# Value and gate transpositions emitted in the middle of the next projection chain

## The chip, the cores and the metric

The kernel runs on one core of a Trainium2 chip. The metric is the device time of that core in microseconds. The engines are PE (matrix products, with PEld for its weight loads), DVE, ACT and POOL (elementwise work), and SP, which issues all of this kernel's DMAs, in order, from one queue.

## The reference

The reference is one transformer block in float32 on 1024 positions of width 1024: a gated feed-forward layer, a mixing layer, a second feed-forward layer and a norm. The mixing layer projects the normed input with one wide matrix and runs two kinds of attention:

```
proj = h @ w_in
(q_da, k_da, v_da, q_ns, kc_raw, vc_raw, ks_raw, vs_raw, kw_raw, vw_raw, g_ns, g_a, g_b) = split(proj)
y_da = diff_attention(q_da, k_da, v_da, ...)          # 8 heads, values 128 wide
y_ns = nsa(q_ns, kc_raw, ..., vw_raw, g_ns, ...)      # 16 heads, 3 branches, gates
merged = sigmoid(g_a) * (y_da @ w_proj_da) + sigmoid(g_b) * (y_ns @ w_proj_nsa)
return merged @ w_out
```

What matters here are the values `v_da` (differential attention), `vs_raw` and `vw_raw` (two branches of the second attention) and the gates `g_ns`. They are computed with the channel on the partitions and are needed with the position on the partitions, so they are transposed.

## The kernel before

Every float32 product is done in three products of rounded parts: high weight by high input, high by low, low by high (`mm3`, lines 49 to 51). A *chain* is the 24 such matmuls that give one tile of 128 channels by 512 positions: 8 blocks of the width, 3 each. The positions are handled in two halves, `tb` 0 and 1.

The *preliminary units* (from 667 us) each load one or two weight tiles, split them on ACT (high part, line 86) and DVE (low part, line 82), run a chain for each half, and finish it:

- `raw_unit` stores the inputs of a compression; `rope_pair` does queries and keys: products with cosines and sines on DVE, sums on POOL, a split into `rh` and `rl`, and stores.
- `v_da_unit` (values of one head of the differential attention) scales the chain's result into `vt` (line 570), transposes it on PE in four pieces into `tr` (line 573), splits it into `vh` and `vl`, and stores both (line 578).
- `v_ns_unit` does the same for the second attention (lines 588 and 591), `g_unit` for the gates (lines 623 and 626), with an exponential and a reciprocal behind it.

`prelim` runs these up to the queries of the second attention; between them stand the compression products (`hid`, lines 700 to 702). `da_phase` first runs six more units (two for heads 0 and 1, four for heads 2 and 3, the last two of them value units), then opens the buffers of the attention and goes through the heads. There each step computes scores `S` (line 791, two buffers), their maximum on DVE (line 798) and exponentials `Pt` on ACT (line 800), transposes the probabilities (line 846) and multiplies them with values (`o`, lines 868 to 870). Between the steps a *filler* (`K.fill`) emits pieces of the remaining projection units, with weights loaded at line 1057 and split at line 1067.

In `v_da_unit` the tile `vt` has the tag `m13`, `vh` the tag `rh` and `vl` the tag `rl` of a pool with one buffer a tag; `rope_pair` uses the same tags. So a `vh` can be written only when the store of the `vh` or `rh` before it has landed.

The program's order is not the order on the engines: the framework's scheduler sorts the instructions by their place in the program (as a priority) and by its own estimate of times, and then each engine works through its list in order. Buffers are assigned in the same step.

Of the kernel before, what the change touches and what calls it, by code (L numbers as in the profile page):

```python
# [7 lines left out]
F32 = mybir.dt.float32  # L8
F32R = mybir.dt.float32r
AF = mybir.ActivationFunctionType  # L10
ALU = mybir.AluOpType
# [4 lines left out]
P = 128  # L16
T = 1024
TB = 512
NTB = 2
HB = 256  # L20
D = 1024
KD = 8
# [25 lines left out]
def mm3(nc, out, w, wk, x, start, stop, skip=False):  # L48
    first = nc.tensor.matmul(out, lhsT=w[0][:, wk], rhs=x[0], start=start, stop=False, skip_group_check=skip)  # L49
    nc.tensor.matmul(out, lhsT=w[0][:, wk], rhs=x[1], start=False, stop=False, skip_group_check=skip)  # L50
    nc.tensor.matmul(out, lhsT=w[1][:, wk], rhs=x[0], start=False, stop=stop, skip_group_check=skip)  # L51
    return first
# [6 lines left out]
def fill_gemm(K, out, w, xs):  # L59
    for k in range(KD):  # L60
        if K.low:
            with K.tc.high_priority(offset=-K.low):
                first = mm3(K.nc, out, w, k, xs[k], k == 0, k == KD - 1)
        else:
            first = mm3(K.nc, out, w, k, xs[k], k == 0, k == KD - 1)
        if K.gate is not None:
            K.tc.add_manual_dep(first.ins, K.gate.ins.name,
                                mybir.DependencyInfo(mybir.DependencyClass.NoSync, mybir.DependencyReason.DATA),
                                reason="pace the filler")
        if K.fill is not None:  # L70
            K.fill.tick(first)
        yield


def drain(units):
    for u in units:
        for _ in u:
            pass


def lo_of(nc, lo, src, hi):
    return nc.vector.tensor_tensor(out=lo, in0=src, in1=hi.bitcast(F32), op=ALU.subtract)  # L82


def split(nc, hi, lo, src):
    nc.scalar.activation(out=hi, in_=src, func=AF.Copy)  # L86
    return lo_of(nc, lo, src, hi)


def load_w(K, src):  # L90
    if K.fill is not None:
        return K.fill.take()
    return load_w_parts(K, src, 1)()
# [469 lines left out]
def v_da_unit(K, h):  # L563
    nc = K.nc
    w = load_w(K, K.A["win"][C_VDA + h])
    for tb in range(NTB):
        ps = K.gm.tile([P, TB], F32, tag="gm", name="gm")
        yield from fill_gemm(K, ps, w, K.h[tb])
        vt = K.mp.tile([P, TB], F32, tag="m13", name="vt")
        nc.vector.tensor_tensor(out=vt, in0=ps, in1=K.R[tb], op=ALU.mult)  # L570
        tr = K.gm.tile([P, 4, P], F32, tag="gm", name="tr")
        for j in range(4):
            nc.tensor.transpose(tr[:, j], vt[:, j * P:(j + 1) * P], K.ident)
        vh = K.mp.tile([P, 4, P], F32R, tag="rh", name="vh")
        vl = K.mp.tile([P, 4, P], F32R, tag="rl", name="vl")
        split(nc, vh, vl, tr)
        for hl, t in ((0, vh), (1, vl)):
            nc.sync.dma_start(out=K.s_v[h][hl][:, tb * 4:tb * 4 + 4], in_=t.bitcast(F32))


def v_ns_unit(K, br):
    nc = K.nc
    w = load_w(K, K.A["win"][C_V2 + br])
    for tb in range(NTB):
        ps = K.gm.tile([P, TB], F32, tag="gm", name="gm")
        yield from fill_gemm(K, ps, w, K.h[tb])
        vt = K.mq.tile([P, TB], F32, tag="vt", name="vt")
        nc.vector.tensor_tensor(out=vt, in0=ps, in1=K.R[tb], op=ALU.mult)
        tr = K.tr.tile([P, 4, P], F32, tag="tr", name="tr")
        for j in range(4):  # L590
            nc.tensor.transpose(tr[:, j], vt[:, j * P:(j + 1) * P], K.ident)
        vv = K.mq.tile([P, 2, 4, 2, 64], F32R, tag="vv", name="vv")
        for g in range(2):
            split(nc, vv[:, g, :, 0], vv[:, g, :, 1], tr[:, :, g * 64:(g + 1) * 64])
            nc.sync.dma_start(out=K.s_v2[br][g][:, tb * 4:tb * 4 + 4],
                              in_=vv[:, g].rearrange("p j a d -> p j (a d)").bitcast(F32))


def raw_unit(K, kv, w=None):
# [16 lines left out]
def g_unit(K):  # L616
    nc = K.nc
    w = load_w(K, K.A["win"][C_G])
    for tb in range(NTB):
        ps = K.gm.tile([P, TB], F32, tag="gm", name="gm")  # L620
        yield from fill_gemm(K, ps, w, K.h[tb])
        vt = K.mq.tile([P, TB], F32, tag="vt", name="vt")
        nc.vector.tensor_tensor(out=vt, in0=ps, in1=K.R[tb], op=ALU.mult)
        tr = K.tr.tile([P, 4, P], F32, tag="tr", name="tr")
        for j in range(4):
            nc.tensor.transpose(tr[:, j], vt[:, j * P:(j + 1) * P], K.ident)
        gs = K.G[:, tb * 4:tb * 4 + 4]
        nc.scalar.activation(out=gs, in_=tr[:, :, 0:48], func=AF.Exp, scale=-1.0)
        nc.vector.tensor_scalar(out=gs, in0=gs, scalar1=1.0, scalar2=None, op0=ALU.add)
        nc.vector.reciprocal(out=gs, in_=gs)  # L630
    for i in range(8):
        nc.vector.tensor_scalar(out=K.Gc[:, i], in0=K.G[:, i].rearrange("p (h b) -> p h b", b=3)[:, :, 0],
                                scalar1=K.rowv[:, i:i + 1], scalar2=None, op0=ALU.mult)


def gate_unit(K, c):
# [558 lines left out]
def da_units(K, p):  # L1195
    return [lambda: rope_pair(K, C_QDA + 2 * p, K.s_q[p]), lambda: rope_pair(K, C_KDA + 2 * p, K.s_k[p]),
            lambda: v_da_unit(K, 2 * p), lambda: v_da_unit(K, 2 * p + 1)]
# [27 lines left out]
def da_phase(K, cg):  # L1225
    nc = K.nc
    with ExitStack() as ctx:
        K.kp, K.vp, K.qp = open_pool(K, ctx, "dk", B_DK), open_pool(K, ctx, "dv", B_DV), open_pool(K, ctx, "dq", B_DQ)
        K.nk, K.vv = {}, {}
        for n, f in enumerate(da_units(K, 0)[:2] + da_units(K, 1)):  # L1230
            if n == 2:
                early = da_load_parts(K, 0)
            if n >= 2:
                next(early)
            if n == 5:
                q0 = da_queries(K, 0, 0)
            drain([f()])
        cg.close()
        K.low = LOW_DA
        log_exp(K)  # L1240
        K.pp, K.sm, K.tp, K.op = (open_pool(K, ctx, "dp", B_DP), open_pool(K, ctx, "dsm", 6), open_pool(K, ctx, "dt", B_DT),
                                  open_pool(K, ctx, "do", 1))
        K.sp = open_pool(K, ctx, "sp1", 2, True)
        K.tr = open_pool(K, ctx, "tr1", TR_DA, True)
        K.ops = open_pool(K, ctx, "o1", 1, True)
        K.gm = open_pool(K, ctx, "gm1", 3 - TR_DA, True)
        pend = K.fin = None

        def finish(h, m, res):
            if m % 2 == 0:  # L1250
                K.o = K.ops.tile([P, TB], F32, tag="o", name="o")
            if K.fin:
                da_finish2(K, *K.fin)
                K.fin = None
            da_pv(K, h, m, res, K.o)
            if m % 2 == 1:
                K.fin = da_finish(K, h, m // 2, K.o)

        ng = NG_DA // 2
        W = K.A["win"]  # L1260
        units = []
        for p in (2, 3):
            cs = [[C_QDA + 2 * p, C_QDA + 2 * p + 1], [C_KDA + 2 * p, C_KDA + 2 * p + 1], [C_VDA + 2 * p], [C_VDA + 2 * p + 1]]
            units += [(f, [W[c] for c in ws]) for f, ws in zip(da_units(K, p), cs)]
        units += [(f, [W[C_GATE + c]]) for c, f in enumerate(gate_units(K, range(16)))]
        units += [(lambda d=d: pda_unit(K, d), [K.A["wda"][d]]) for d in range(KD)]
        fill = K.filler = Filler(K, units)
        for p in range(4):
            fill.pace(4 * (p + 1) if p < 2 else 8 + ng * (p - 1), PACE_DA)
            for h in (2 * p, 2 * p + 1):  # L1270
                if h:
                    da_load(K, h)
                for m in range(4):
                    qt = q0 if h + m == 0 else da_queries(K, h, m)
                    if h == 4:
                        ns_load_key(K, m)
                    res = da_scores(K, h, m, qt, fill.step)
                    if pend:
                        finish(*pend)
                    pend = (h, m, res)  # L1280
            fill.end()
        finish(*pend)
        da_finish2(K, *K.fin)
# [108 lines left out]
def body(tc, A, out):  # L1392
    nc = tc.nc
    K = Ctx()
    K.tc, K.nc, K.A = tc, nc, A
    K.low, K.vv, K.gate, K.fill, K.seen = 0, {}, None, None, {}
    K.h, K.acc, K.R = [None] * 2, [None] * 2, [None] * 2
    with ExitStack() as ctx:
# [172 lines left out]
```

## Time and profile before

| | us |
|---|---|
| median of 3 runs | 2966.28 |
| lowest, highest | 2965.57, 2974.5 |
| profiled execution | 2967.67 |
| its span in the trace | 2965.9 |
| busy: PE / DVE / ACT / POOL | 2862.2 / 1974.1 / 1268.8 / 975.4 |
| mean granted clock of PE | 0.991 |

PE is busy for 97% of the span, at close to full clock. The busy times are sums over stages that differ, so what an idle time is worth has to be read in its own stage. In the trace a row of a timeline names the line, the engine, the tiles written and read, and in brackets how long the engine had stood idle before and what released it.

### The profile page before, as it was taken

Reading aid. Unit: us, or ns where it says so; the run is one execution under the profiler, and the core shown is the slowest. Engines: PE = TensorE matmul, PEld = TensorE weight load, DVE = VectorE, ACT = ScalarE, POOL = GpSimd, SP = SyncE. Lnnn points to the kernel's source line nnn. Section 1 sums busy time; section 2 is a strip of 40 time slices with the busy share of each in tenths; the row PEclk is TensorE's granted clock in tenths of the full one; section 3 lists DMA queues with packets and bytes.
Section 4 is the critical chain, followed back from the end, with each engine's and each line's share of the span. In section 5 each row is a group of like instructions: output and inputs, shape, how many; then the busy total and the mean of one; then the engine's idle time right before and its main releaser. Section 6 shows DMA issues by size and latency. Waiting matters only on the chain.

```text
span 2965.9 us, 39981 instructions
## 1 busy us (share of the span) xinstructions
PE 2862.2 (97%) x14238; PEld 2392.2 (81%) x14238; DVE 1974.1 (67%) x3140; ACT 1268.8 (43%) x2195; POOL 975.4 (33%) x765
## 2 busy tenths in 40 slices
PE   9999999999999899989899999999999999999998
PEld 7877878888888678778788888888778888778886
DVE  8775666666587467667777777776433866676556
ACT  6322224442233245445566666666433432223343
POOL 4366651000144123222233332223242436655001
PEclk9999999999999999999999999999999999999999
DMA  4355557655456544444332234222742145455854
GB/s 139 114 190 180 181 196 273 216 179 171 151 199 222 184 162 164 175 165 163 127 122 70 85 127 154 79 82 72 299 148 96 64 149 206 163 178 197 280 181 147
DMA packets 212711, 478.19 MB, mean 161 GB/s; under 512 B 20897, under 2 KB 39585, under 8 KB 212513
## 3 DMA queue, kind: packets, MB, share of 16 engines
q1 hardware_dynamic: 212512, 475.65, 47.0%
q8 instruction: 112, 1.84, 0.3%
q14 instruction: 87, 0.70, 0.1%
HBM read 313.56 MB, written 162.00 MB: 160 GB/s over the span
## 4 chain that ended last, share of the span: by engine, by line
PE 68%; DMA 11%; DVE 9%; POOL 4%; issue 4%; ACT 3%; SPq 1%; DVEq 0%; ACTq 0%; POOLq 0%
PE gm L49 6%; PE S L791 6%; PE gm L50 6%; PE gm L51 6%; PE Y L324 5%; PE acc L51 5%; PE acc L49 5%; PE acc L50 5%; PE tr L846 4%; PE X L324 3%; PE Z L324 3%; PE o L1004 2%; DVE w2s L432 2%; PE o L1003 2%; DVE wlo L82 2%
## 5 line engine op out<-in xcount | busy, mean ns | idle before, releaser
L49 PE MATMUL gm<-hi,whi 128*128 128x512 f32 x880 | 351.6, 400 | 4.0 <-ACT whi L86 1.9
L51 PE MATMUL gm<-hi,wlo 128*128 128x512 f32 x880 | 348.3, 397 | 0.2 <-DVE wlo L82 0.2
L50 PE MATMUL gm<-lo,whi 128*128 128x512 f32 x880 | 348.3, 396 | 0.0
L791 PE MATMUL S<-kt,qt 128*128 128x320 f32 (+5 forms) x1152 | 274.6, 352 | 34.6 <-ACT Pt L800 10.3
L82 DVE TENSOR_TENSOR tl<-tr,th 128x512 fp32r<-128x512 f32 (+2 forms) x384 | 236.3, 619 | 84.4 <-ACT th L86 80.9
L86 ACT ACTIVATE th<-tr 128x512 fp32r<-128x512 f32 (+2 forms) x384 | 203.7, 542 | 201.7 <-PE tr L846 195.8
L324 PE MATMUL Y<-tf,whi 128*128 128x512 f32 x864 | 270.7, 395 | 8.4 <-DVE u L367 5.4
L82 DVE TENSOR_TENSOR wlo<-st,whi 128x1024 fp32r<-128x1024 f32 x154 | 197.7, 1302 | 117.7 <-ACT whi L86 117.2
L798 DVE CUSTOM_DVE_ANT_0 S<-S,slab 128x896 f32<-128x896 f32 (+7 forms) x320 | 224.6, 709 | 65.4 <-PE S L791 59.8
L50 PE MATMUL acc<-wlo,whi 128*128 128x512 f32 (+1 forms) x628 | 242.8, 387 | 0.0
L49 PE MATMUL acc<-whi 128*128 128x512 f32 (+1 forms) x628 | 242.6, 386 | 0.0
L51 PE MATMUL acc<-whi,wlo 128*128 128x512 f32 (+1 forms) x628 | 242.3, 388 | 0.0
L86 ACT ACTIVATE whi<-st 128x1024 fp32r<-128x1024 f32 x154 | 160.0, 1057 | 187.2 <-PE acc L51 114.6
L957 POOL TENSOR_SCALAR Ps<-Ps,l 128x384 f32<-128x384 f32 (+7 forms) x128 | 100.7, 787 | 423.3 <-DVE l L955 208.7
L791 PEld LDWEIGHTS S<-kt,qt 128*128 128x128 f32 x1152 | 183.2, 190 | 58.9 <-ACT Pw L800 12.9
L324 PEld LDWEIGHTS Y<-tf,whi 128*128 128x128 f32 x864 | 162.2, 189 | 48.6 <-issue 7.4
L49 PEld LDWEIGHTS gm<-hi,whi 128*128 128x128 f32 x880 | 168.3, 191 | 37.0 <-ACT whi L86 2.1
L51 PEld LDWEIGHTS gm<-hi,wlo 128*128 128x128 f32 x880 | 167.9, 191 | 36.5 <-DVE wlo L82 0.7
L50 PEld LDWEIGHTS gm<-lo,whi 128*128 128x128 f32 x880 | 168.1, 191 | 31.0
L82 DVE TENSOR_TENSOR wlo<-a,whi 128x1024 fp32r<-128x1024 f32 x90 | 138.1, 1536 | 80.4 <-ACT whi L86 80.1
L324 PE MATMUL Y<-tf,wlo 128*128 128x512 f32 x432 | 170.2, 395 | 0.0
L1003 PE MATMUL o<-th,vt 128*128 128x256 f32 (+1 forms) x608 | 164.5, 287 | 1.8 <-ACT th L86 1.7
(314 smaller groups left out, 7004.0 us busy)
## 6 DMA issues: line engine op xcount, KB each, us to landing
wst<-in_win_dram SPq DMA_DIRECT2D x55, 512.0 KB
sw<-w2s SPq DMA_DIRECT2D x44, 512.0 KB
st<-sw SPq DMA_DIRECT2D x88, 256.0 KB
st<-saT SPq DMA_DIRECT2D x88, 256.0 KB
a<-in_f1w_dram SPq DMA_DIRECT2D x36, 512.0 KB
a<-in_f2w_dram SPq DMA_DIRECT2D x36, 512.0 KB
st<-saB SPq DMA_DIRECT2D x66, 256.0 KB
qt<-sq SPq DMA_DIRECT2D x128, 128.0 KB
```

What stands on the lines that cost most here:

```text
L49: first = nc.tensor.matmul(out, lhsT=w[0][:, wk], rhs=x[0], start=start, stop=False, skip_group_check=skip)
L50: nc.tensor.matmul(out, lhsT=w[0][:, wk], rhs=x[1], start=False, stop=False, skip_group_check=skip)
L51: nc.tensor.matmul(out, lhsT=w[1][:, wk], rhs=x[0], start=False, stop=stop, skip_group_check=skip)
L82: return nc.vector.tensor_tensor(out=lo, in0=src, in1=hi.bitcast(F32), op=ALU.subtract)
L86: nc.scalar.activation(out=hi, in_=src, func=AF.Copy)
L324: K.mark = nc.tensor.matmul(o, lhsT=w[a][:, m * h + k], rhs=x[k][b], start=start and k == 0 and i == 0, stop=k == h - 1 and i == 2, skip_g ...
L432: nc.vector.tensor_tensor(out=out, in0=a, in1=b, op=op)
L791: K.last = nc.tensor.matmul(S[:, o:o + n], lhsT=q, rhs=k[:, k0 + c:k0 + c + n], start=i == 0, stop=i == 1)
L798: nc.vector.tensor_tensor_reduce(out=sv, in0=sv, in1=mv, scale=-0.125, scalar=BIG, op0=ALU.add, op1=ALU.min, accum_out=nm)
L846: nc.tensor.transpose(tr[:, b * P:(b + 1) * P], src, K.ident)
L957: nc.gpsimd.tensor_scalar(out=p[:, 0:n], in0=p[:, 0:n], scalar1=l[:, c:c + 1], scalar2=1.0, op0=ALU.mult, op1=ALU.mult)
L1003: nc.tensor.matmul(dst, lhsT=v, rhs=hi[:, b * P:(b + n) * P], start=False, stop=False, skip_group_check=True)
```

## The change

In `fill_gemm` a list of pending functions is worked off in the middle of a chain (after the block k = 4) when no filler runs. The three units hand over what follows the copy `vt` (transpositions, split, stores, or the gates' exponential) instead of doing it at once: `later` runs it immediately inside a filler unit, and otherwise puts it on the list. A call before the buffers of the preliminary stage are closed works off the last one.

```diff
         if K.fill is not None:
             K.fill.tick(first)
+        elif k == KD // 2:
+            flush(K)
         yield
+
+
+def later(K, f):
+    if K.fill is not None:
+        f()
+    else:
+        K.late.append(f)
+
+
+def flush(K):
+    late, K.late = K.late, []
+    for f in late:
+        f()
...
@@ v_da_unit
         nc.vector.tensor_tensor(out=vt, in0=ps, in1=K.R[tb], op=ALU.mult)
-        tr = K.gm.tile([P, 4, P], F32, tag="gm", name="tr")
-        for j in range(4):
-            nc.tensor.transpose(tr[:, j], vt[:, j * P:(j + 1) * P], K.ident)
-        vh = K.mp.tile([P, 4, P], F32R, tag="rh", name="vh")
-        vl = K.mp.tile([P, 4, P], F32R, tag="rl", name="vl")
-        split(nc, vh, vl, tr)
-        for hl, t in ((0, vh), (1, vl)):
-            nc.sync.dma_start(out=K.s_v[h][hl][:, tb * 4:tb * 4 + 4], in_=t.bitcast(F32))
+        def rest(tb=tb, vt=vt):
+            tr = K.gm.tile([P, 4, P], F32, tag="gm", name="tr")
+            for j in range(4):
+                nc.tensor.transpose(tr[:, j], vt[:, j * P:(j + 1) * P], K.ident)
+            vh = K.mp.tile([P, 4, P], F32R, tag="rh", name="vh")
+            vl = K.mp.tile([P, 4, P], F32R, tag="rl", name="vl")
+            split(nc, vh, vl, tr)
+            for hl, t in ((0, vh), (1, vl)):
+                nc.sync.dma_start(out=K.s_v[h][hl][:, tb * 4:tb * 4 + 4], in_=t.bitcast(F32))
+        later(K, rest)
...
@@ v_ns_unit, g_unit: the same, with the split and the stores, or the gates' work, inside rest()
...
@@ da_phase, after the six units
             drain([f()])
+        flush(K)
         cg.close()
```

The line numbers of the changed kernel are higher by 15 to 24 in these functions. Nothing else is changed in the program, but the scheduler's lists differ from here on. They are the same up to about 757 us. From there to about 800 us (value units 0 and 1) and from about 1008 to about 1400 us they differ; behind that they agree again. The transpositions of gates and of the second attention's values (lines 591 and 626) stand at the same places on PE as before. Numbers behind a name tell buffers apart; of two lists the same number is not always the same tile.

On PE, at the entry of the attention phase (value units 2 and 3; `gm` are their chains, `tr` their transpositions, `S` the scores), before:

```order
L791 MATMUL S_8368<-kt_7919,qt_8356 128x384 x2
L573 MATMUL tr_8096<-ident_299,vt_8094 128x128 x4
L49 MATMUL gm_8107<-hi_5236,whi_8064 128x512
...
L791 MATMUL S_8412<-kt_7775,qt_8353 128x512 x2
L791 MATMUL S_8418<-kt_7919,qt_8356 128x512 x2
L573 MATMUL tr_8134<-ident_299,vt_8132 128x128 x4
L49 MATMUL gm_8159<-hi_4491,whi_8154 128x512
...
L791 MATMUL S_8469<-kt_7775,qt_8460 128x320 x4
L791 MATMUL S_8477<-kt_7919,qt_8463 128x320 x4
L573 MATMUL tr_8186<-ident_299,vt_8184 128x128 x4
```

and in the changed kernel, where the chain of the second half of unit 2 already stands ahead of these rows:

```order
L589 MATMUL tr_8112<-ident_299,vt_8094 128x128 x4
L49 MATMUL gm_8148<-hi_4491,whi_8143 128x512
...
L589 MATMUL tr_8164<-ident_299,vt_8132 128x128 x4
L49 MATMUL gm_8186<-hi_5236,whi_8143 128x512
...
L589 MATMUL tr_8202<-ident_299,vt_8184 128x128 x4
L813 MATMUL S_8418<-kt_7919,qt_8356 128x512 x2
L813 MATMUL S_8469<-kt_7775,qt_8460 128x320 x4
L589 MATMUL tr_8224<-ident_299,vt_8222 128x128 x4
L813 MATMUL S_8477<-kt_7919,qt_8463 128x320 x4
L813 MATMUL S_8518<-kt_7775,qt_8460 128x384 x4
```

The transpositions now have a chain or scores between them and the chain that they belong to, the chains stand one place earlier against the scores, and two more scores stand between tr_8224 and the next chain.

On ACT at the same place (`vh` the copies of the transposed values, `Pt` the exponentials, `whi` a weight's high part), before:

```order
L800 ACTIVATE Pt_8361,l_8359<-S_8362,nm_8360 128x384
L86 ACTIVATE vh_8101<-tr_8096 128x512
L800 ACTIVATE Pt_8367,l_8359<-S_8368,nm_8360 128x384
L1067 ACTIVATE whi_8281<-wst_8279 128x1024
L800 ACTIVATE Pt_8411,l_8409<-S_8412,nm_8410 128x512
L86 ACTIVATE vh_8139<-tr_8134 128x512
L800 ACTIVATE Pt_8417,l_8409<-S_8418,nm_8410 128x512
L800 ACTIVATE Pt_8468,l_8466<-S_8469,nm_8467 128x640
L86 ACTIVATE vh_8191<-tr_8186 128x512
L800 ACTIVATE Pt_8476,l_8466<-S_8477,nm_8467 128x640
L1067 ACTIVATE whi_8287<-wst_8285 128x1024
L800 ACTIVATE Pt_8517,l_8515<-S_8518,nm_8516 128x768
```

and in the changed kernel:

```order
L101 ACTIVATE vh_8117<-tr_8112 128x512
L822 ACTIVATE Pt_8361,l_8359<-S_8362,nm_8360 128x384
L822 ACTIVATE Pt_8367,l_8359<-S_8368,nm_8360 128x384
L101 ACTIVATE vh_8169<-tr_8164 128x512
L822 ACTIVATE Pt_8411,l_8409<-S_8412,nm_8410 128x512
L1089 ACTIVATE whi_8287<-wst_8285 128x1024
L101 ACTIVATE vh_8207<-tr_8202 128x512
L822 ACTIVATE Pt_8417,l_8409<-S_8418,nm_8410 128x512
L101 ACTIVATE vh_8229<-tr_8224 128x512
L128 ACT_TABLE_LOAD
L822 ACTIVATE Pt_8468,l_8466<-S_8469,nm_8467 128x640
L822 ACTIVATE Pt_8476,l_8466<-S_8477,nm_8467 128x640
```

All four copies vh now stand ahead of Pt_8468, where two stood before; vh_8229 and a table load, which stood behind the last row shown of before, have moved to just ahead of it.

On SP, later in the attention phase (`kt` keys, `qt` queries, `sv` stores of values of a filler unit), before:

```order
L924 DMA kt_10623<-skv_84 128x1x1024
L908 DMA kt_11124<-sk2_78 128x1x1024
L810 DMA qt_10758<-sq2_74 128x1x256 x2
L908 DMA kt_11126<-sk2_78 128x1x1024
L578 DMA sv6_0_97<-vh_10374 128x512
L578 DMA sv6_1_98<-vl_10375 128x512
```

and in the changed kernel:

```order
L594 DMA sv6_0_97<-vh_10374 128x512
L832 DMA qt_10755<-sq2_74 128x1x256
L594 DMA sv6_1_98<-vl_10375 128x512
L1079 DMA wst_10394<-in_win_dram 128x1024
L832 DMA qt_10755<-sq2_74 128x1x256
L946 DMA kt_10623<-skv_84 128x1x1024
L930 DMA kt_11124<-sk2_78 128x1x1024
```

The store of vh_10374 stood behind the key loads and now stands ahead of them.

## Rows read from the trace of the kernel before

**Rows 1.** Busy by stretch: length, PE, PEld, DVE, ACT, POOL, PEclk, DMA share, GB/s

```profile
667.00:960.00 293.00, 288.39 (x1453) 243.65 (x1452) 212.01 (x322) 92.63 (x128) 81.01 (x61) 0.99 0.56 186
960.00:1060.00 100.00, 86.46 (x391) 70.97 (x391) 49.60 (x92) 26.31 (x47) 16.66 (x16) 0.95 0.48 163
...
1190.00:1300.00 110.00, 96.18 (x478) 80.73 (x477) 71.55 (x144) 46.66 (x99) 32.37 (x32) 0.91 0.49 174
```

**Rows 2.** Who PE waited for, preliminary stage: us, times, longest

```profile
PE gm L49 <- ACT whi L86: 1.9, 1, 1.9
PE tr L626 <- DVE vt L623: 1.6, 1, 1.6
PE tr L573 <- DVE vt L570: 1.0, 2, 0.6
```

**Rows 3.** The same at the start of the attention phase

```profile
PE S L791 <- ACT Pt L800: 9.1, 7, 4.3
PE tr L573 <- DVE vt L570: 4.8, 2, 2.6
```

**Rows 4.** Timeline of PE at the entry: start, us, instruction, idle time before

```profile
1014.56 0.86 PE L791 MATMUL S<-kt,qt 128*128 128x384 f32 x4
1018.05 0.65 PE L573 MATMUL tr<-ident,vt 128*128 128x128 f32 x4 [2.63 <-DVE vt L570]
...
1024.88 0.73 PE L791 MATMUL S<-kt,qt 128*128 128x512 f32 x2 [0.22 <-ACT Pt L800]
1027.75 0.66 PE L573 MATMUL tr<-ident,vt 128*128 128x128 f32 x4 [2.15 <-DVE vt L570]
...
1043.85 1.07 PE L791 MATMUL S<-kt,qt 128*128 128x448 f32 x4 [1.07 <-ACT Pt L800]
```

**Rows 5.** Timeline of ACT there

```profile
1023.66 0.60 ACT L86 ACTIVATE vh<-tr 128x512 fp32r<-128x512 f32 x1 [4.44 <-DMA sk<-rh]
...
1029.08 0.59 ACT L86 ACTIVATE vh<-tr 128x512 fp32r<-128x512 f32 x1
...
1035.51 0.80 ACT L800 ACTIVATE Pt<-S,nm 128x640 f32<-128x640 f32 x1 [5.18 <-DVE nm L798]
...
1036.29 0.59 ACT L86 ACTIVATE vh<-tr 128x512 fp32r<-128x512 f32 x1
...
1044.31 1.28 ACT L113 ACT_TABLE_LOAD   x1
```

**Rows 6.** Timeline of SP's DMA issues there

```profile
1024.29 0.33 SPq L578 DMA_DIRECT2D sv<-vh  x1
...
1030.72 0.55 SPq L578 DMA_DIRECT2D sv<-vl  x1
```

**Rows 7.** Timeline of DVE there

```profile
1038.00 0.69 DVE L82 TENSOR_TENSOR vl<-tr,vh 128x512 fp32r<-128x512 f32 x1 [1.81 <-DMA sv<-vl]
```

**Rows 8.** The chain that ended last: start, us, what

```profile
172.88 2.65 DMA sw<-w2s
```

**Rows 9.** Timeline of SP's DMA issues inside the attention phase

```profile
1257.66 4.93 SPq L908 DMA_DIRECT2D kt<-sk  x1
1262.69 1.58 SPq L578 DMA_DIRECT2D sv<-vh  x1
```

**Rows 10.** Timeline of ACT there

```profile
1259.44 0.60 ACT L86 ACTIVATE vh<-tr 128x512 fp32r<-128x512 f32 x1
...
1275.37 0.60 ACT L86 ACTIVATE vh<-tr 128x512 fp32r<-128x512 f32 x1 [4.20 <-DMA sv<-vh]
```

**Rows 11.** Timeline of PE there

```profile
1276.59 1.22 PE L791 MATMUL S<-kt,qt 128*128 128x512 f32 x2 [4.26 <-ACT Pt L800]
```

**Rows 12.** Busy time by stretch of 4 us, columns as in rows 1

```profile
1016.00:1020.00 4.00, 1.95 (x11) 1.69 (x12) 2.93 (x7) 0.67 (x2) 0.00 (x0) 1.00 0.99 348
...
1276.00:1280.00 4.00, 3.41 (x13) 3.12 (x14) 2.94 (x8) 2.08 (x7) 0.00 (x0) 0.50 0.27 97
1280.00:1284.00 4.00, 4.00 (x14) 3.16 (x13) 1.24 (x3) 0.77 (x3) 0.58 (x1) 0.68 0.63 244
```

More of the change, by code (lines that the diff above doesn't have):

```diff
@@ L588, in v_ns_unit, with rest @@
         nc.vector.tensor_tensor(out=vt, in0=ps, in1=K.R[tb], op=ALU.mult)
[L589 to L596, printed above, removed]
+        def rest(tb=tb, vt=vt):
+            tr = K.tr.tile([P, 4, P], F32, tag="tr", name="tr")
+            for j in range(4):
+                nc.tensor.transpose(tr[:, j], vt[:, j * P:(j + 1) * P], K.ident)
+            vv = K.mq.tile([P, 2, 4, 2, 64], F32R, tag="vv", name="vv")
+            for g in range(2):
+                split(nc, vv[:, g, :, 0], vv[:, g, :, 1], tr[:, :, g * 64:(g + 1) * 64])
+                nc.sync.dma_start(out=K.s_v2[br][g][:, tb * 4:tb * 4 + 4],
+                                  in_=vv[:, g].rearrange("p j a d -> p j (a d)").bitcast(F32))
+        later(K, rest)
 def raw_unit(K, kv, w=None):
@@ L623, in g_unit, with rest @@
         nc.vector.tensor_tensor(out=vt, in0=ps, in1=K.R[tb], op=ALU.mult)
[L624 to L633, printed above, removed]
+        def rest(tb=tb, vt=vt):
+            tr = K.tr.tile([P, 4, P], F32, tag="tr", name="tr")
+            for j in range(4):
+                nc.tensor.transpose(tr[:, j], vt[:, j * P:(j + 1) * P], K.ident)
+            gs = K.G[:, tb * 4:tb * 4 + 4]
+            nc.scalar.activation(out=gs, in_=tr[:, :, 0:48], func=AF.Exp, scale=-1.0)
+            nc.vector.tensor_scalar(out=gs, in0=gs, scalar1=1.0, scalar2=None, op0=ALU.add)
+            nc.vector.reciprocal(out=gs, in_=gs)
+            if tb == NTB - 1:
+                for i in range(8):
+                    nc.vector.tensor_scalar(out=K.Gc[:, i], in0=K.G[:, i].rearrange("p (h b) -> p h b", b=3)[:, :, 0],
+                                            scalar1=K.rowv[:, i:i + 1], scalar2=None, op0=ALU.mult)
+        later(K, rest)
 def gate_unit(K, c):
@@ L1395, in body @@
     K.tc, K.nc, K.A = tc, nc, A
+    K.late = []
     K.low, K.vv, K.gate, K.fill, K.seen = 0, {}, None, None, {}
```

## The prediction

> **What bounds the kernel now.** I read the stretches first, then who waited for whom on TensorE (PE), then the engines' timelines where it waited. [Rows 1] shows the stage of the change: in the preliminary stage (667 to 960 us) PE is busy 288.39 of 293 us, so at most 4.6 us can be had there; in the 100 us in which the attention phase starts it is busy 86.46, and in 1190 to 1300, inside that phase, 96.18 of 110, at a granted clock of 0.91. The end is set by PE; only its idle time and the stretches at half clock can be gained. [Rows 2] is all that PE waited for in the preliminary stage: three groups, of which only the last, 1.0 us, is a transposition of values of differential attention. [Rows 3] has the same group in the attention phase's first part: 4.8 us in two waits, and beside it a larger sum, 9.1 us, in which the scores S wait for the exponentials Pt of the buffer before.
>
> **The change, part by part.** No arithmetic is added: 14 groups of four transpositions with their split into high and low part and their stores are emitted later. The list of instructions is sorted by a scheduler, so I read its result. *Gates and values of the second attention (six groups):* their places on PE are the same as before, since the scheduler had already put other chains ahead of them. They change nothing; the 1.6 us of [rows 2] stays, and so does the 1.9 us wait for a weight.
>
> *Value units 0 and 1 (four groups).* The two waits of together 1.0 us [rows 2] go: each transposition now has a later chain, or compression products, between it and the copy vt that it needs. What could be late next is the weight split that moves behind the second vh copy on ACT; its chain comes more than a chain of 24 matmuls later, so I cost it at nothing (if that cover is gone, a wait like the 1.9 us one). Term: -1.0.
>
> *Value units 2 and 3, at the entry of the attention phase (four groups).* Before, PE has four idle times here [rows 4]: 2.63, 0.22, 2.15 and 1.07 us, in sum 6.07. From the start of the scores at 1014.56 to the end of those at 1043.85 + 1.07 = 1044.92 pass 30.36 us, so 24.29 are work. In the new order the same chains and transpositions stand before the first attention filler (tile gm_8295), without S_8526 (four products of 384 columns, 0.86 as the first row of [rows 4]) and without S_8617 (its last row, 1.07). So 22.36 us of work lie before it, and without a wait PE would stand at S_8518, the last 0.86 of these, at 1014.56 + 22.36 - 0.86 = 1036.1.
>
> There it will wait. S has two buffers, so S_8518 needs Pt_8468, which reads the buffer. In the new order ACT does Pt_8468 only behind the copies vh_8117, vh_8169, vh_8207, vh_8229 and a table load. The four vh share one buffer (tag rh of a pool with one buffer), so each has to wait until the store of the one before has landed. Before, other work lay between them: they started at 1023.66, 1029.08 and 1036.29 (a fourth follows) [rows 5], and only the first waited for a DMA (the store of rh, which doesn't move). Now PE delivers the last two close together. With s for a store's time from issue to landing: between tr_8202 and 1036.1 lie S_8418, S_8469, tr_8224 and S_8477, some 2.7 us by the durations of [rows 4] less their overlap, so vh_8207 is written at about 1033.4; SP issues its store behind a query load that waits for S_8418, at about 1034; vh_8229 can start at 1034 + s, takes 0.60, the table load 1.28, Pt_8468 (128x640) 0.80 [rows 5]. S_8518 starts at about 1036.7 + s, and the wait is 0.6 + s.
>
> What is s? No row times one alone. By [rows 5, 6] the first store was issued at 1024.29, and the next copy started at 1029.08 without waiting for it, so s was at most 4.8. A store of the low part, issued at 1030.72 behind a weight load, held its successor until 1038.00 [rows 6, 7]: 7.3. A store twice as large in a quieter stage took 2.65 [rows 8]. Ends 2.65 and 7.3; I take 4.2, near the bound of the same store (4.8) since the queue now holds a weight load and query loads here too. The wait is then 4.8 against 6.07 taken away: -1.3. At 2.65 the term is -2.8; at 7.3 each of the four copies slips (vh_8169 at 1031.6, vh_8207 at 1039.5, vh_8229 at 1047.4, S_8518 at 1050.1), the wait is 14.0, and the term is +7.9.
>
> The Trainium skill (DMA: Bandwidth & Descriptors, section Anatomy of one DMA) gives a DMA about 2 us that don't depend on size, most of it until the write is acknowledged, and bytes at 436 GB/s. An estimate by it for 256 KB is 2.6 us, with which the entry term would be -2.9; its remark that this delay can be surprisingly long for writes to HBM speaks against four such stores in a row. The 7.3 us of [rows 7] shows that here a store can take far longer than that estimate.
>
> One long wait costs more than itself: after the idle 4.26 us before 1276.59 the clock stood at 0.50 and 0.68 for two stretches of 4 us [rows 11, 12], which is 0.50 x 4 + 0.32 x 4 = 3.3 us of lost work. After 2.63 us at 1018 it stayed at 1.00 [rows 4, 12]. The present waits cost no clock, the new one of 4.8 probably does; I take 3.0. Term of the entry: -1.3 + 3.0 = +1.7, with ends -2.8 and +7.9 + 3.3 = +11.2.
>
> *The rest of the attention phase, to about 1420.* The scheduler orders it anew, with the same instructions. One wait has a visible cause that moves: at 1259.44 ACT writes a vh, but its store is issued only at 1262.69, behind a key load that held SP for 4.93 us; the next vh waits 4.20 us for that store and PE 4.26 us behind it [rows 9 to 11]. In the new order this store stands ahead of those key loads. It can be issued at 1260.0 instead of 1262.69: 2.6 us less of the wait. I take -2.0 (ends 0, since ACT may then meet the next such store, and -4.3 - 3.3 = -7.6 with its clock). The other waits there I take as exchanged for equal ones, with 5 us to either side, about one long wait with half of its clock. After that the order is that of before, and PE is ahead or behind by what came until then.
>
> Sum: -1.0 + 1.7 - 2.0 = -1.3 us. The profiled execution took 2967.67 us, 1.77 outside its span, and lies 1.4 above the median of the runs, 2966.28. On the median's scale I forecast 2965.0.
>
> **Rivals.** *Slower: the stores in a row decide.* The four vh at the entry, and the vh of the filler units, which now stand a few instructions earlier on ACT than the exponentials, find their single buffer taken. For it: the 7.3 us [rows 7] and the 4.20 us [rows 10]. Against: the copies before waited for none of their own stores at the entry [rows 5]. It decides when a store takes over 5 us. Price: +11.2 less 1.0: +10, so 2976.
>
> *Faster: the waits are really gone.* Stores take some 2.65 us; then the wait at S_8518 is 3.3 and may leave the clock up: -2.8 for the entry, -1.0, and -7.6 for the wait at 1276 with its clock: -11.4, so 2955. For it: the copies at 1029.08 and 1036.29 didn't wait [rows 5]. Against: ACT's order ahead of Pt_8468.
>
> *No effect.* Six of 14 groups don't move, and what the others free is taken by the next dependence; 2966. It can't be told from the forecast by time, only by the trace.
>
> **How the numbers follow.** A measurement of this kernel tells about 0.3% (8.9 us) from no change. Forecast with no effect: 0.65, its own range 2959 to 2972. Slower rival 0.19, faster rival 0.16. Below 2957.4 falls most of the faster rival: 0.14. Above 2975.2 most of the slower: 0.17. Within: 0.69. The range for 8 in 10 reaches into both: 2955 to 2976, which takes in both ends of the store's time except the worst of it with every other wait turned against it.
>
> **What would show it.** Right: no wait of the value transpositions for vt in 667 to 1060 except that of the gates; a PE wait of 3 to 6 us at the scores of 768 columns near 1037 to 1041, released by Pt on ACT, with vh waiting for the store of vh before it, and half clock after it; the wait near 1276 shorter. Wrong: no such wait at the entry (the faster rival), or vh copies that wait over 5 us each (the slower one); or stretches before 750 or behind 1420 whose length differs by more than 2 us, where no order moves.

## The result, and the profile after

The change costs 0.6%, some 18 us, where the forecast was no change.

| | us, median (lowest to highest, runs) | profiled execution | span | mean clock |
|---|---|---|---|---|
| before | 2970.03 (2965.57 to 2974.50, 4) | 2967.67 | 2965.9 | 0.991 |
| after | 2989.62 (2986.01 to 2991.65, 4) | 2989.07 | 2987.3 | 0.988 |

Ratio 1.0061, 95% interval 1.0044 to 1.0078. The time lies outside the predicted range (2955 to 2976), on the side to which the prediction gave 0.17.

First the stretches of the changed kernel, with the columns of [rows 1]:

```profile
667.00:960.00 293.00, 288.03 (x1458) 243.21 (x1457) 212.66 (x325) 93.22 (x129) 81.10 (x62) 1.00 0.56 186
960.00:1060.00 100.00, 86.52 (x388) 71.73 (x387) 46.10 (x85) 24.66 (x44) 16.31 (x16) 0.91 0.47 158
...
1190.00:1300.00 110.00, 95.08 (x478) 78.34 (x477) 73.99 (x148) 47.13 (x99) 29.98 (x29) 0.95 0.46 163
1300.00:1420.00 120.00, 108.68 (x568) 92.49 (x567) 80.55 (x170) 58.54 (x122) 28.58 (x29) 0.94 0.45 153
```

The first three answer to [rows 1] and hardly differ from it. The fourth does; it was before:

```profile
1300.00:1420.00 120.00, 116.54 (x630) 99.36 (x629) 89.11 (x190) 64.90 (x133) 29.57 (x32) 1.00 0.47 160
```

568 matmuls stand against 630 in the same stretch, and the clock is lower. The loss sits where the prediction hardly looked. The next two rows hold the part of the attention phase whose order the change touches, in before and in after: the same matmuls but for a missing record.

```profile
1008.70:1383.88 375.18, 348.87 (x1798) 293.48 (x1797) 263.13 (x537) 177.47 (x364) 101.25 (x100) 0.97 0.48 167
```
```profile
1010.36:1401.42 391.06, 354.27 (x1797) 297.25 (x1795) 265.31 (x534) 176.28 (x361) 103.61 (x100) 0.95 0.46 159
```

391.06 less 375.18 is 15.9 us: idle time of PE grew from 26.3 to 36.8 (10.5), and the same matmuls were busy 5.4 longer, at a lower clock.

To find the places I compare both traces at equal work: for each moment of before, the start in the other kernel of the matmul that has as many columns behind it (both move 5,953,528 in all). How far a kernel is behind before, less what it was at 1000 us (worked out from the traces; one execution each):

```
us of before       1060    1260    1300    1320    1360    1380    1400    1560
after             -0.03    0.89    0.87    9.60    8.93   15.27   16.16   19.15
entry_only         1.89    3.67    3.85   12.21   11.11   16.13   16.98   16.91
values_first       1.40    2.52    2.78    7.42    6.90   12.15   13.01   16.49
values_first2      0.32   -1.61   -2.26    5.15    3.84    5.94    6.17    9.14
scores_first       1.85    3.80    3.93    3.90    3.83    3.83    5.96    7.17
one_score_first    1.96    1.97    3.34    3.40    2.44    2.44    2.56    3.69
order_back         2.23    2.13    5.11    5.11    4.84    4.84    4.90    5.10
scores_later      -0.69   -2.38   -2.14    5.73    4.42    9.38    9.96    9.80
order_late        -0.01    0.31   -0.25   -0.42   -0.35    4.92    5.88   10.06
two_buf_before    -0.19   -2.99   -0.86   -0.88   -0.53   -0.53   -0.80   -0.99
prelim_only        0.97    4.03    4.42    4.40    4.37    4.37    6.20    7.38
```

The other lines are the experiments below. prelim_only has before's order on PE from 798 us on, and still ends 7.4 us behind in its one profiled execution, the slowest of its 11: a line is to be read for its steps, and a step under some 4 us says nothing alone. In after there are two above that: 8.7 us between 1300 and 1320 and 6.3 between 1360 and 1380. The 3.0 behind 1400 lie under it and are not shown to be the change's: prelim_only, in before's order, loses 3.0 behind 1380. At the entry, over which the prediction worked hardest, this trace has no step.

PE of the changed kernel ahead of and at these two places (its times lie 2 to 17 us behind those of before):

```profile
1288.14 1.22 PE L813 MATMUL S<-kt,qt 128*128 128x512 f32 x2 [3.83 <-ACT Pt L822]
...
1293.46 0.47 PE L49 MATMUL gm<-hi,whi 128*128 128x512 f32 x1 [2.39 <-DVE l L852]
...
1316.18 0.55 PE L890 MATMUL o<-th,vt 128*128 128x256 f32 x1 [4.36 <-DMA vt<-sv]
...
1318.39 0.58 PE L892 MATMUL o<-th,vt 128*128 128x256 f32 x1 [1.44 <-DMA vt<-sv]
...
1372.34 0.36 PE L890 MATMUL o<-th,vt 128*128 128x256 f32 x1 [1.89 <-ACT Pt L822]
...
1373.66 0.58 PE L892 MATMUL o<-th,vt 128*128 128x256 f32 x1 [0.84 <-DMA vt<-sv]
```

At 1316 and 1372 begin the products of heads 4 and 5 with values vt. Before, PE waited less at both:

```profile
1295.11 0.36 PE L868 MATMUL o<-th,vt 128*128 128x256 f32 x1 [2.82 <-DMA vt<-sv]
...
1359.16 0.39 PE L870 MATMUL o<-th,vt 128*128 128x256 f32 x1 [0.48 <-DMA vt<-sv]
```

The windows show what followed in the changed kernel:

```profile
1316.00:1320.00 4.00, 2.38 (x10) 2.11 (x11) 0.00 (x0) 0.00 (x0) 0.00 (x0) 0.50 0.52 180
1320.00:1324.00 4.00, 4.00 (x15) 3.20 (x15) 2.81 (x6) 2.00 (x4) 0.91 (x1) 0.78 0.26 100
1372.00:1376.00 4.00, 2.81 (x12) 2.55 (x13) 0.00 (x0) 0.84 (x3) 2.17 (x3) 0.62 0.40 139
1376.00:1380.00 4.00, 4.00 (x12) 3.19 (x11) 3.03 (x5) 1.10 (x2) 0.00 (x0) 0.53 0.16 56
```

In the second and fourth window PE never stops, at a clock of 0.78 and 0.53: 0.9 and 1.9 us of work are lost there after the wait is over.

### The profile page after: what moved, and what is told of

It reads as the page before. It is cut to its first block, busy times and chain, and to the rows that moved or that the text cites. A ratio compares the mean times of both kernels' runs of the same rounds, so it can differ in the third digit from the quotient of the medians.

```text
span 2987.3 us, 39983 instructions
## 1 busy us (share of the span) xinstructions
PE 2867.5 (96%) x14238; PEld 2395.8 (80%) x14238; DVE 1981.2 (66%) x3140; ACT 1267.9 (42%) x2195; POOL 978.0 (33%) x765
## 4 chain that ended last, share of the span: by engine, by line
PE 43%; DMA 6%; DVE 6%; issue 3%; ACT 2%; POOL 2%; SPq 1%; DVEq 0%; ACTq 0%; POOLq 0%
PE S L813 5%; PE tr L868 3%; PE gm L49 3%; PE gm L51 3%; PE gm L50 3%; PE acc L51 2%; PE acc L49 2%; PE acc L50 2%; PE o L1026 2%; PE Y L339 2%; PE o L1025 2%; DVE w2s L447 1%; DMA w2s<-in_f2w_dram 1%; PE Z L339 1%; PE X L339 1%
## 5 line engine op out<-in xcount | busy, mean ns | idle before, releaser
L339 PE MATMUL Y<-tf,whi 128*128 128x512 f32 x864 | 271.6, 396 | 10.5 <-DVE u L382 7.8
```

Of the source, the lines that this page charges most:

```text
L339: K.mark = nc.tensor.matmul(o, lhsT=w[a][:, m * h + k], rhs=x[k][b], start=start and k == 0 and i == 0, stop=k == h - 1 and i == 2, skip_g ...
```

## The experiments

Each was timed in five rounds against before on the same chip; 1.0010 is 3.0 us.

| kernel | the change in it | ratio (95% interval) | median, before beside it |
|---|---|---|---|
| prelim_only | in the preliminary stage only | 0.9995 (0.9987 to 1.0004) | 2968.49, 2970.72 |
| entry_only | at the entry only | 1.0044 (1.0032 to 1.0056) | 2984.79, 2970.72 |
| scores_first | whole, before's order behind the entry | 1.0010 (1.0002 to 1.0019) | 2975.87, 2970.72 |
| one_score_first | whole, a third order | 0.9999 (0.9990 to 1.0008) | 2966.40, 2966.44 |
| order_back | whole, before's order from 1280 us | 1.0028 (1.0016 to 1.0039) | 2975.11, 2966.70 |
| scores_later | none, after's order behind the entry | 1.0040 (1.0027 to 1.0053) | 2981.57, 2970.72 |
| order_late | none, after's order from 1305 us | 1.0023 (1.0014 to 1.0033) | 2974.45, 2966.70 |
| low24 | none, another priority of the filler | 1.0013 (1.0004 to 1.0021) | 2969.83, 2966.70 |
| values_first | whole, value loads of head 4 earlier | 1.0045 (1.0032 to 1.0058) | 2979.76, 2966.44 |
| values_first2 | whole, those of heads 4 and 5 | 1.0045 (1.0031 to 1.0058) | 2980.72, 2968.52 |
| two_buf | as scores_first, second vh/vl buffer | 0.9997 (0.9987 to 1.0006) | 2966.17, 2966.44 |
| two_buf_before | none, second vh/vl buffer | 0.9999 (0.9990 to 1.0008) | 2967.18, 2966.44 |
| two_buf_q5 | none, and a fifth query buffer | 0.9999 (0.9991 to 1.0008) | 2966.22, 2966.70 |
| buffers | preliminary stage, both buffers | 0.9995 (0.9986 to 1.0003) | 2964.62, 2966.70 |
| head4_first | buffers, value loads of head 4 first | 0.9995 (0.9987 to 1.0004) | 2966.76, 2968.14 |
| head4_first2 | the same behind a query load | 0.9986 (0.9978 to 0.9995) | 2963.76, 2968.14 |

**Which part.** The list of kept-back work is used in one stage only; a flag set at the head of the attention phase decides (shown for prelim_only; entry_only has `or not K.entry`):

```diff
-    if K.fill is not None:
+    if K.fill is not None or K.entry:
         f()
     else:
         K.late.append(f)
```

prelim_only. 

> Only the preliminary stage has the change; value units 2 and 3 are emitted as before, and TensorE's order behind 800 us is that of before. Theory A (the time is lost in the new order of the attention phase behind its entry): within 2 us of before, -0.5 to -2 us (the two waits of 1.0 us are gone, the trace of the changed kernel had gained 1.8 us by 800 us). Theory B (the kept-back groups themselves cost it, by their stores one behind the other): about +2 to +5 us, since two of the four value units are kept back. Theory C (a difference of the runs before 667 us or behind 1420 us): the +5 us that the trace of the changed kernel shows there stay.

entry_only. 

> Only value units 2 and 3 are kept back, at the entry of the attention phase; the preliminary stage is that of before, and the order behind the entry is that of the changed kernel. Theory A: all of the loss, +15 to +20 us on before (about 1.006). Theory B: +13 to +16. Theory C: under +12. It tells A from B only together with the next two kernels.

The loss comes with value units 2 and 3 (the intervals of entry_only and of the whole change overlap); the preliminary part shows no loss.

**Kept-back work or new order.** At the entry the new order puts the filler's first chain ahead of two buffers of scores that stood before it, and the scores stay one chain later for some 200 us. An edge of order (no wait between engines) undoes that in the changed kernel, and another does it in the kernel before. `K.calls` counts the buffers of scores; `first0` is the first matmul of the filler, `chain0` stands for its first chain; NTH is 13 in scores_first, where the first piece belongs, and 12 in scores_later:

```diff
+            K.calls += 1
+            if K.calls == NTH:
+                K.tc.add_manual_dep(K.first0.ins, K.last.ins.name,
...
```
```diff
+            if K.calls == NTH - 1 and i == 0 and o == 0 and K.fill is None and K.chain0 is not None:
+                order_after(K, K.last, K.chain0)
```

scores_first. 

> The whole change, with one edge of order added: the filler's first chain stands behind the scores that it had behind it in the kernel before. The entry is that of the changed kernel; from some 50 us behind it on, TensorE's order is again that of before. Theory A: the loss is gone, -3 to +4 us on before. Theory B: the entry and its stores are the same, so the loss stays, +10 to +20 us. Theory C: +5 us stay.

scores_later. 

> The kernel before without any of the change, with one edge of order added: the scores of one buffer stand behind the filler's first chain, after which the order of the attention phase is nearly that of the changed kernel. Theory A: it loses what the changed kernel loses, +12 to +20 us on before. Theory B: nothing is kept back, so 0 within 3 us. Theory C: 0 within 3 us.

one_score_first (scores_first with NTH = 12). 

> The whole change, with the filler's first chain held behind one buffer of scores less than in scores_first. The entry is the same; a third order of the attention phase follows, the same instructions, equal to the order of before only from some 230 us behind the entry on (index 5706 of TensorE). Theory A: another time in between, and its difference from scores_first lies behind the entry: 0 to +15 us on before. If the cost were in the kept-back groups and not in the order behind them, it would equal scores_first and the changed kernel within 3 us.

Theory A holds. scores_later keeps nothing back; in the traces PE's order in it is that of before up to 1041 us and from there to the end that of the changed kernel, to the last instruction, and it loses 12 us. scores_first keeps everything back, has the same entry, is back in before's order from about 1096 us, and loses 3. one_score_first does the same work in a third order for nothing. Theory B, the prediction's slower rival in which stores in a row decide, falls with it as the cause of the loss. So does C: the differences outside the attention phase that I had seen in one trace did not come with the kept-back work. What is shown is the new order as a whole; with PE's list those of SP and ACT change, and these runs don't tell them apart.

**From which place.** The same kind of edge between the 69th buffer of scores and the filler's 24th chain (order_late), or the 67th and the 23rd (order_back):

order_back. 

> The whole change; TensorE's order is that of the changed kernel through the entry and on to index 5603 (about 1250 us), where one edge holds a filler chain behind one buffer of scores, and from index 5705 (about 1280 us) on it is that of before. Theory A1 (the loss comes at the places behind 1280 us, where heads change, by the order there): 0 to +5 us on before. Theory A2 (the 200 us in which the scores run one chain later make it): +10 to +18.

order_late. 

> The kernel before without the change; its order holds through the entry to index 5677 (about 1268 us), where one edge puts one buffer of scores behind a filler chain, and from index 5825 (about 1305 us) on the order is that of the changed kernel. Theory A1: +6 to +13 us on before, lost at the change to heads 4 and 5. Theory A2: within 3 us of before.

Neither half has it all. With the changed order up to 1250 it is 8.3 us, of which the table of equal work finds 5.1, in steps too small to place (2.2 at the entry, 3.0 between 1260 and 1300). With the changed order from 1305 it is 6.8 us; the table puts 5.3 at 1360 to 1380 and 4.2 behind 1400, where the order is again that of before. The step at 1300 to 1320 appears only in the kernels that have the changed order on both sides of it. I had expected one place; it is several.

**What is late at these places.** SP issues all loads and stores in order. The last product of head 3 in the changed kernel, then SP ahead of the wait at 1316, then the value loads in before:

```profile
1302.12 0.28 PE L892 MATMUL o<-th,vt 128*128 128x128 f32 x1
```
```profile
1299.09 5.64 SPq L832 DMA_DIRECT2D qt<-sq  x2
1304.82 0.72 SPq L666 DMA_DIRECT2D smx<-vt  x1
1305.64 2.62 SPq L937 DMA_DIRECT2D vt<-sv  x2
```
```profile
1287.77 0.79 SPq L915 DMA_DIRECT2D vt<-sv  x2
```

The values of one head fill the pool, so those of head 4 can be loaded once the last product of head 3 has ended, at 1302.4. At that moment SP stands in a query load, and the two value loads are out only at 1308.26. Before, they were out within a microsecond of the last product (ended 1287.85).

```diff
+            if h in VFIRST and m == 3 and c == 1:
+                order_after(K, ld, K.vld)
```

Here `ld` is a query load and `vld` the second value load; VFIRST is (4,), and (4, 5) in values_first2.

values_first. 

> The changed kernel with one edge on SP's queue: the two value loads of head 4 are issued ahead of the last query load of that head (four places on SP), TensorE's order is the same to the last instruction. In the changed kernel the last product that needs their buffer ended at 1302.4, the loads were issued at 1307.8 behind query loads that waited, and TensorE waited 4.36 + 1.44 us for them, with half clock for 6.8 us (3.4 us). Theory A1 (the place on the queue makes that wait): issued 4 to 5 us earlier, the wait falls to 1 to 2 us and its clock stays up: -5 to -8 us on the changed kernel, some +10 to +13 on before. Theory A2 (the load is slow by itself, or the next late thing takes the place): -2 us or less.

```profile
1312.41 0.36 PE L892 MATMUL o<-th,vt 128*128 128x256 f32 x1 [1.08 <-DMA vt<-sv]
...
1313.74 0.39 PE L894 MATMUL o<-th,vt 128*128 128x256 f32 x1 [0.85 <-DMA vt<-sv]
```

With PE's order untouched the loads are out at 1303.73, the waits fall from 5.80 to 1.93 us, and the step at 1300 to 1320 from 8.7 to 4.6. A1, the place on the queue, holds for this place. The time follows by about as much (1.0045 for 1.0061), but these two intervals overlap, so a gain in time is not shown.

values_first2 (head 5 too, ahead of a gate store and a weight load). 

> values_first, and the same for head 5: its two value loads go ahead of a query load, the store of a gate chain and a weight load on SP (TensorE's order stays that of the changed kernel). There the last product that needs their buffer ended at 1359.48 and the loads were issued at 1363.0; TensorE waited 1.89 us (put down to an exponential) and 0.84 us (for the value load), with 6.9 us of half clock. If the value load makes that place too: issued 3 to 4 us earlier, the two waits fall under 1 us together and the clock stays up, -3 to -6 us on values_first (some +8 to +10 on before). If the exponential makes it, or the query load that is now behind: within 2 us of values_first (about +13).

In its trace PE no longer waits at the first products of head 5, and the step at 1360 to 1380 shrinks from 6.3 to 2.1; a query load, now behind, takes 1.15 us in two waits:

```profile
1367.17 0.44 PE L815 MATMUL S<-kt,qt 128*128 128x448 f32 x1 [0.26 <-DMA qt<-sq]
1368.50 0.88 PE L815 MATMUL S<-kt,qt 128*128 128x448 f32 x3 [0.89 <-DMA qt<-sq]
```

The medians don't show it: the ratio is that of values_first. The first place costs 7.4 us again in this trace, with waits of 2.76 and 0.83 us for the same value loads, and the profiled execution (2974.01) was the fastest of five. What the second place is worth stays open.

**The buffer of vh and vl.** Every second copy goes to the tile m42 of the rotary pairs:

```diff
-            vh = K.mp.tile([P, 4, P], F32R, tag="rh", name="vh")
-            vl = K.mp.tile([P, 4, P], F32R, tag="rl", name="vl")
+            if tb:
+                v2 = K.mp.tile([P, 2, 4, P], F32R, tag="m42", name="v2")
+                vh, vl = v2[:, 0], v2[:, 1]
+            else:
+                vh = K.mp.tile([P, 4, P], F32R, tag="rh", name="vh")
+                vl = K.mp.tile([P, 4, P], F32R, tag="rl", name="vl")
```

two_buf. 

> The whole change with the edge of scores_first, and a second buffer for vh and vl (the tile that the rotary pairs use), so that every second store need not be waited for. At the entry TensorE's order is that of the changed kernel up to the scores in question; behind them the order is new again. Theory B' (the wait at the scores at the entry, 4.53 us with its half clock, comes from vh waiting for the store of vh before it): the wait there falls under 2 us and the entry ends 5 to 7 us earlier than in scores_first. If it comes from elsewhere (the table load, the exponentials themselves), it stays over 3 us. Its whole time depends on the new order behind it: -6 to +10 us on before.

PE of two_buf at the entry (the scores in question are the last row):

```profile
1036.60 0.85 PE L818 MATMUL S<-kt,qt 128*128 128x320 f32 x4 [0.78 <-ACT Pt L827]
1038.87 0.66 PE L878 MATMUL tr<-ident,Pt 128*128 128x128 f32 x4 [1.42 <-DVE v L98]
1039.29 0.96 PE L818 MATMUL S<-kt,qt 128*128 128x384 f32 x4
```

The scores for which PE waited 4.53 us wait no more, and half clock doesn't follow (granted 1.00 from 1036 to 1048); 1.42 us stand at a transposition ahead of them. B' is right on the cause. The whole has another order again, and its time is that of before.

two_buf_before. 

> The kernel before without the change, with the second buffer for vh and vl alone; every engine keeps its order. The wait of 4.26 us at 1276.59, which the prediction put down to vh waiting for the store of vh before it, should go with its half clock: -4 to -8 us on before. If it stays, the prediction's reading of that wait was wrong: within 2 us of before.

```profile
1285.92 0.38 PE L795 MATMUL S<-kt,qt 128*128 128x320 f32 x1 [4.25 <-DMA qt<-sq]
1287.27 1.17 PE L795 MATMUL S<-kt,qt 128*128 128x320 f32 x3 [0.96 <-DMA qt<-sq]
1294.07 0.55 PE L872 MATMUL o<-th,vt 128*128 128x256 f32 x1 [4.14 <-DMA vt<-sv]
```

The wait of [rows 11] is gone, as its reading said, and nothing is won: 4.26 and 2.82 us became 5.21 for queries and 4.14 for the values of head 4.

two_buf_q5 (B_DQ = 5). 

> The kernel before with the second buffer for vh and vl and a fifth buffer for the queries; TensorE keeps its order. In two_buf_before the wait of 4.26 us at 1276 was gone, and the scores at 1285.9 waited 4.25 us for a query load that SP had held back for 6.98 us; the time stayed. If that query wait is what took the place of the removed one, it goes now and some of its price shows: -3 to -7 us on before. If the value load behind it (4.14 us at 1294) takes the place again, or another: within 2 us of before.

Who PE waited for in 1190 to 1300 there:

```profile
PE o L872 <- DMA vt<-sv: 11.8, 1, 11.8
PE o L872 <- ACT th L86: 3.5, 1, 3.5
```

Now one wait holds most of them. Whatever was taken away in front, the values of head 4 came late, and PE reached them earlier.

buffers. 

> The part of the change that did no harm (values kept back in the preliminary stage only) with both extra buffers; TensorE's order is that of prelim_only. The candidate for a version that beats both kernels: -1.5 us of prelim_only beside what two_buf_q5 gives, -1 to -9 us on before; if every removed wait is replaced by the next, 0 to -2.

head4_first (value loads ahead of syd, a value store and the query load). 

> The kernel buffers (values kept back in the preliminary stage only, second buffer for vh and vl, fifth query buffer) with edges on SP's queue: the two value loads of head 4 go ahead of a query load, of the output of head 3's first half and of a value store. TensorE's order stays. In buffers all idle time at the change of heads had gathered in one wait of 12.0 us for that load, and in two_buf_q5 the load was issued some 8 us after the last product that holds its buffer. If the place on SP's queue makes the wait: it falls to 3 to 6 us, -5 to -9 us on before. If what is now behind it takes the place (the query load): 0 to -3.

head4_first2. 

> The same with the query load left ahead of the value loads. If the query load holds SP until its buffer is free (in two_buf_q5 it did until 1286), the value loads gain only 3 to 4 us: -2 to -5 us on before. If not, as head4_first.

In head4_first the loads are out at 1284.74 instead of 1288.54 (buffers), and the wait for them falls, in buffers and in head4_first:

```profile
PE o L894 <- DMA vt<-sv: 12.0, 1, 12.0
```
```profile
PE o L898 <- DMA vt<-sv: 8.1, 1, 8.1
```

With the loads out 3.8 us earlier the wait is 3.9 us shorter, not by the 6 to 9 expected. Behind it PE now waits elsewhere (1300 to 1420; in buffers this line has 0.7 us):

```profile
PE gm L49 <- DVE vt L671: 5.8, 2, 3.6
```

head4_first2 is the only version whose interval lies below before, by 4.2 us, and not for the reason expected: in its trace the loads are out later, at 1293.69, and the wait for them is still 10.0 us. That execution (2969.07) was one of the three slowest of twelve, and one of sixteen kernels can come out so by chance; that it is faster, and why, stays open.

**A new order without the change.** LOW_DA = 24 for 20.

low24. 

> The kernel before without the change; only the constant that says how far the filler's priority lies under the rest is 24 in place of 20, which gives another order of the attention phase from some 120 us behind its entry to its end, with the same instructions. If a new order of this phase by itself moves the time (theory A), it differs from before, to either side, by 3 to 20 us; the kernel's constants were set with the old order, so slower is the likelier side. If orders are worth the same within what was taken in the prediction: within 5 us.

It differs by 3.8 us, which lies in both expectations and decides nothing between them: an order can also cost little.

## Why the prediction was wrong

*The step that failed* is the term for the rest of the attention phase: "I take -2.0", and "The other waits there I take as exchanged for equal ones, with 5 us to either side". It measured about +15: after less scores_first, 1.0061 less 1.0010, some 9 to 21 by the two intervals; scores_later, which has this term and nothing else of the change, lost 12. I knew that the scheduler had ordered a stretch of 1800 matmuls anew, priced one wait whose cause I could see, and called the rest an exchange. The orders of these instructions that were timed, most of them made by single edges and the change's own among them, cost 0, 3, 4, 7, 8, 12, 13 and 18 us. No row of before bounds that from above; 5 us to either side had no ground. Of the 15, the late value loads of head 4 are shown as the cause of one wait; how the rest divides stays open.

*The wait at 1276* was misjudged twice. I said the store of vh would stand ahead of the key loads. One store did, at 1258.44. The next met the same key load, and vh waited longer than before (ACT, then SP):

```profile
1286.93 0.60 ACT L101 ACTIVATE vh<-tr 128x512 fp32r<-128x512 f32 x1 [6.82 <-DMA sv<-vh]
```
```profile
1269.22 5.29 SPq L930 DMA_DIRECT2D kt<-sk  x1
1274.62 1.56 SPq L594 DMA_DIRECT2D sv<-vh  x1
```

PE's 4.26 us became the 3.83 at 1288.14. That end of the range had been named. What had not been seen is, first, that the wait was worth nothing by itself, since the value load stood behind it (two_buf_before). Second, most of it was not the hold-up on SP: by [rows 9, 10] the store issued at 1262.69 freed vh at 1275.37, 12.7 us later, and here it is 12.3 (1274.62 to 1286.93), outside the 2.65 to 7.3 that the prediction gave a store at the entry.

*The entry* came out nearly as worked out. Forecast: vh behind vh's stores, a table load, Pt, and a wait of 4.8 us of the scores. Measured:

```profile
1035.34 0.60 ACT L101 ACTIVATE vh<-tr 128x512 fp32r<-128x512 f32 x1 [0.60 <-DMA sv<-vh]
...
1039.19 0.60 ACT L101 ACTIVATE vh<-tr 128x512 fp32r<-128x512 f32 x1 [2.58 <-DMA sv<-vh]
1039.80 1.28 ACT L128 ACT_TABLE_LOAD   x1
1041.10 0.79 ACT L822 ACTIVATE Pt<-S,nm 128x640 f32<-128x640 f32 x1
```
```profile
1036.66 0.85 PE L813 MATMUL S<-kt,qt 128*128 128x320 f32 x4 [0.87 <-ACT Pt L822]
1042.03 1.65 PE L813 MATMUL S<-kt,qt 128*128 128x384 f32 x4 [4.53 <-ACT Pt L822]
```
```profile
1042.00:1046.00 4.00, 3.97 (x12) 3.45 (x13) 3.43 (x7) 1.75 (x4) 0.80 (x1) 0.59 0.22 80
```

5.40 us of idle time took the place of the 6.07 of [rows 4], and 0.41 x 4 = 1.6 us of work went to the clock: +1.0 where +1.7 was forecast. The table of equal work gives 0.0 to 2.2 for the kernels with this entry. By the runs it isn't settled: scores_first less prelim_only is 1.0015, 4.5 us, with an interval that reaches down to about 1, and one_score_first, which has the same entry, costs nothing. A store's time s, taken as 4.2, was 6.0 and 3.2 here: issued at 1029.35 and 1035.96, waited for until 1035.34 and 1039.19. The estimate by the Trainium skill (DMA: Bandwidth & Descriptors, Anatomy of one DMA) was 2.6; both measurements lie above it, and below the 7.3 of [rows 7]. That section gives its fit for DMAs issued by GpSimd, and these stores are issued by SP.

*The preliminary stage* was right: no value transposition waits there (only the gates', 2.4 us, and weight waits of together 2.5); prelim_only is 1.5 us faster than before, with an interval that takes in no change.

*The signs to look for* did their work except one: "stretches before 750 or behind 1420" were to differ by under 2 us. Behind 1400 a further 3.0 us went although the order there is that of before: at the entry of the next stage PE waited 2.52 us for th (at 1489.89), with half clock behind it. prelim_only, in before's order, lost 3.0 behind 1380, so a limit of 2 us lies below what single executions differ by.

## What to carry to other kernels

A change in program order under a scheduler is two changes: what it moves, and the order that is found for everything behind. The second has no sign and can be the larger; ask how far the new order reaches before pricing a single wait, take its range from the idle time that the phase has, and separate the two with one edge of order. Where several engines feed one, a wait is worth only what lies between it and the next late thing: here a value load that could not start before the head before it had ended. And price a transfer by when its last part lands behind what is queued with it, not by its size.

## What the runs showed of the hardware that I had not expected

Taking PE's wait away twice lengthened the wait behind it each time, until 11.8 us stood in one place at no loss: before's several waits with half clock between them cost as much as one. And the transfers of this phase are slow to be usable: in two_buf_q5 a value load of 512 KB issued at 1289.49 let PE go at 1297.85, 8.4 us, and in the changed kernel 10.1 us passed from the end of the issue at 1308.26 to the first product with the second value tile at 1318.39.

The times at which parts of a transfer land, which the trace also has, show where this comes from. In the changed kernel between 1258 and 1310 us each query and key load lands in four parts, beside one update at its issue, and each store and each load of values or weights in sixteen. Of the store issued at 1274.62, twelve parts had landed at 1277.83, the last four between 1285.73 and 1286.85, just before vh was written; of the value load issued at 1307.88, twelve by 1313.28, the last four between 1315.42 and 1318.35, just before PE used it. While the last parts of that store were outstanding, about a quarter of the 16 DMA engines was busy (last two columns: share, GB/s):

```profile
1282.00:1286.00 4.00, 2.07 (x14) 1.47 (x12) 2.11 (x6) 0.00 (x0) 0.00 (x0) 1.00 0.26 103
```

At the entry in before, the store issued at 1024.29, with no other DMA issued in the 7 us ahead of it, landed whole by 1026.33, 2.0 us. So the stores and value loads seem to wait for four of their parts behind the queries and keys, which use a quarter of the engines. No run here tests that; query loads that land in sixteen parts would be the experiment.
